# Causal pooling of three groups by transposes and doubled sums on VectorE instead of banded products

## The chip, the cores and the metric

The kernel runs on one core of one Trainium2 chip. The metric is the time of one execution on the device, in microseconds (us), as the median of several runs; lower is better. Each run is one layer of a decoder on 256 tokens of 2048 channels, in fp32.

A core has a matrix engine (TensorE, PE in the profile), a vector engine (VectorE, DVE), a scalar engine (ScalarE, ACT), a general engine (GpSimd, POOL) and a queue engine that issues most transfers (SyncE, SP). Each engine takes its own list of instructions in order, and semaphores tie the lists together. Products are summed in PSUM, a memory of eight banks.

## The reference

One input product gives, for each token, q, k, v, z (2048 columns each), two small sets for the heads, the pooling input p, and two gates g_a and g_b. q, k and v go through a causal convolution and then the gated delta rule (`gated_delta_rule`), whose output is normalized per head and gated by z. Beside it runs the pooling, in four groups of 512 channels with windows 2, 4, 8 and 16:

```
def causal_multiscale_pool(u):        # u: (B, S, G, Cg)
    cs = jnp.pad(jnp.cumsum(uf, axis=1), ((0, 0), (1, 0), (0, 0), (0, 0)))
    t = jnp.arange(seq)
    for gi, win in enumerate(POOL_WINDOWS):
        hi = cs[:, 1:, gi]
        lo = cs[:, jnp.maximum(t + 1 - win, 0), gi]
        cnt = jnp.minimum(t + 1, win).astype(jnp.float32)
        outs.append((hi - lo) / cnt[None, :, None])
    ...
    return (pooled - uf)
...
y_b = jnp.einsum('bsgc,gcd->bsgd', pooled, pool_w[l]).reshape(bsz, seq, D_POOL) * pool_scale[l]
mixed = jax.nn.sigmoid(g_a) * y_a + jax.nn.sigmoid(g_b) * y_b
```

So each token gets the mean over its last `win` tokens less itself, times a 512x512 matrix per group (`pool_w`). The rest of the layer is the output product and a gated MLP with 5632 hidden channels.

## The kernel before, in words

**Weights.** All matrices are fp32 and are used as two parts, a high part `whi` and a low part `wlo`. A weight tile is 256 rows by 512 columns. `srcs` lists all tiles in the order of use; SP issues their loads into four buffers `raw`; ScalarE casts `raw` to `whi` (L143) and VectorE subtracts it from `raw` to give `wlo` (L151), here called the split. `whi` and `wlo` have three buffers each. The activations are held in two parts too (`xhl`). `gemm_a` (L170 to L185) multiplies one tile into a pair of PSUM banks (`psm`) by 12 products of 128x512: high by high (L181), low by high (L182), high by low (L183), for two halves of the rows and two halves of the tokens. A product of 2048 rows takes eight tiles, one of `pool_w` two. There are two pairs of `psm` and four single banks `psg`.

**Order.** Work on the side is put between the weight products in two ways. Functions put into `later` run when the second tile of the next `gemm_a` begins. And after every six products `side()` takes one step of a generator, `gdn` (from L634), which holds the gated delta rule of the group: decays, gram products of q and k, the inverses of 32x32 blocks by many small VectorE steps (L744, L746), their doubling by small products, and the output. Each `yield` ends a step, and `LATE` and `WAIT` are counts of empty steps. The order in which each engine takes its instructions is then set by the build's planner, which goes by its own estimates of time and is not bound to the order of the text; only the start and, on PE, group 3's end are ordered by hand.

**Groups.** The loop at L864 runs over four groups of 512 channels. Each one multiplies k, q, v, p and the gate g_b, then `pool_w`, then z and g_a. Every result is scaled and evicted from PSUM to the tile `ev` by ScalarE (`evict`). k and q are turned (channels to partitions) by eight transposes on PE (`turned`, L226) and convolved there. v stays with tokens in the partitions; its convolution adds three copies moved by one to three tokens, which go through a DRAM tile (`vrow` stored at L883, `mv` loaded at L594, multiplied by the taps at L601, added at L602).

**Pooling.** `pooled` (L894 to L905) multiplies the evicted p by a band matrix (`bands`, one per group) that holds the mean's weights, 1/win or one over the count at the start, less the identity. It takes eight fp32 products (L899, L901), which the profile lists as two records each; the result is turned as it comes. ScalarE casts it to `phi` (L904) and VectorE takes `plo` from PSUM (L905), two halves each. The bands are made once by GpSimd and VectorE in `fixed_parts` (L534 to L548). The product with `pool_w` follows g_b's; its result is scaled by `pool_scale` (L918), then by one plus the tanh of g_b (L919). z's gate goes to `sz` (L923).

**The 0/1 product.** The normalization of q within the rule needs sums of q's squares per head and token. They are summed over 32 columns (`qp`, L725), then a product with a 0/1 matrix `sel` (L729) brings the parts together into `psg`, and four VectorE instructions (L733) scale them into `ro`, which the rule's end reads (L857). This stands ahead of the inverses' steps.

Of the kernel before, what the change touches and what calls it, by code (L numbers as in the profile page):

```python
# [7 lines left out]
F32 = mybir.dt.float32  # L8
# [5 lines left out]
P = 128  # L14
S = 256
# [19 lines left out]
def kernel(  # L35
# [492 lines left out]

    bands = mp.tile([P, 4, NB], F32, name="bands")

# [3 lines left out]
    def fixed_parts():  # L534
        for g, win in enumerate(WINDOWS):
            bd = bands[:, g, :]
            nc.gpsimd.memset(bd, 0.5 / win)
            nc.vector.tensor_copy(bd[:, 0:PAD], icnt[:, g, :])
            for cs in (slice(0, P + PAD), slice(P + PAD, NB)):
                b = bd[:, cs]  # L540
                n = cs.stop - cs.start
                nc.gpsimd.affine_select(b, b, pattern=[[1, n]], compare_op=ALU.is_ge, fill=0.0, base=0,
                                        channel_multiplier=-1)
                nc.gpsimd.affine_select(b, b, pattern=[[-1, n]], compare_op=ALU.is_ge, fill=0.0, base=win - 1,
                                        channel_multiplier=1)
                nc.vector.tensor_tensor(b[:, 0:P], b[:, 0:P], idh, op=ALU.subtract)
        nc.gpsimd.memset(Ta, 0.0)
        nc.gpsimd.memset(TTa, 0.0)  # L548
# [85 lines left out]
    def gdn(g, kq, vt, conv, res):  # L634
# [92 lines left out]
        yield  # L727
        pn = pg([P, 4, 2, 4])
        mm(pn.rearrange("p h t c -> p (h t c)"), sel.rearrange("p b i -> p (b i)"), qp, start=True, stop=True)  # L729
        ro = mp.tile([P, 2, 4], F32, tag="ro", name=nm("ro"))  # L730
        for c in range(4):
            pr = slice(32 * c, 32 * c + 32)
            nc.vector.tensor_scalar(ro[pr], pn[pr, :, :, c].rearrange("p h t -> p t h"), EPS * P, EPS * EPS * P,  # L733
                                    op0=ALU.mult, op1=ALU.add)
        for _ in range(WAIT - 3 + LATE[g]):
# [128 lines left out]
    for g in range(4):  # L864
# [24 lines left out]
        ps = gemm_a(xh, xl, KD)  # L889
        e = evict(ps)  # L890
        phi = mtile(g, [P, 4, S], F32R, nm("phi"))
        plo = mtile(4 + g, [P, 4, S], F32R, nm("plo"))

        def pooled(e=e, g=g, phi=phi, plo=plo):  # L894
            for f2 in range(2):
                pt = pg([P, 2, S])
                for ff in range(2):
                    fs = slice((2 * f2 + ff) * P, (2 * f2 + ff + 1) * P)
                    mm(pt[:, ff, P:S], e[:, 1, fs], bands[:, g, P + PAD : NB], start=True, stop=False,  # L899
                       skip_group_check=True)  # L900
                    mm(pt[:, ff, 0 : P + PAD], e[:, 0, fs], bands[:, g, 0 : P + PAD], start=False, stop=True,  # L901
                       skip_group_check=True)
                fs = slice(2 * f2, 2 * f2 + 2)
                nc.scalar.copy(phi[:, fs, :], pt)  # L904
                nc.vector.tensor_tensor(plo[:, fs, :], pt, phi[:, fs, :].bitcast(F32), op=ALU.subtract)  # L905

        later.append(pooled)

# [14 lines left out]
        nc.vector.scalar_tensor_tensor(sz, gate(ps, "th"), 1.0, ps, op0=ALU.add, op1=ALU.mult)  # L923
        if g == 3:
# [220 lines left out]
```

## Time and profile before

| | |
|---|---|
| median of 3 runs | 1565.36 us (1564.85 to 1565.47) |
| the profiled execution | 1565.06 us |
| its span in the profile | 1563.3 us |
| granted TensorE clock | 0.998 |
| PE busy | 1554.1 us, 99% |
| VectorE busy | 1085.6 us, 69% |
| ScalarE busy | 745.7 us, 48% |
| GpSimd busy | 41.3 us, 3% |
| read from HBM | 297.56 MB, 194 GB/s over the span |

The profile is one execution as the hardware profiler saw it. Its rows name a line of the kernel, an engine, an operation, and tiles in the form out<-in; a tile's name without its number stands for all of that name. In the views by time, a row has the start and the duration in us; x2 or x8 means that so many alike follow one another. Matmuls overlap: the time from one start to the next is shorter than the duration of one. The share of a DMA or engine is an average over the stretch named. "Idle before" is the time in which an engine had nothing to do just before an instruction, with what ended it.

### The profile page before, as it was taken

Reading aid. Unit: us, or ns where it says so; the run is one execution under the profiler, and the core shown is the slowest. Engines: PE = TensorE matmul, PEld = TensorE weight load, DVE = VectorE, ACT = ScalarE, POOL = GpSimd, SP = SyncE. Lnnn points to the kernel's source line nnn. Section 1 sums busy time; section 2 is a strip of 40 time slices with the busy share of each in tenths; the row PEclk is TensorE's granted clock in tenths of the full one; section 3 lists DMA queues with packets and bytes.
Section 4 is the critical chain, followed back from the end, with each engine's and each line's share of the span. In section 5 each row is a group of like instructions: output and inputs, shape, how many; then the busy total and the mean of one; then the engine's idle time right before and its main releaser. Section 6 shows DMA issues by size and latency. Waiting matters only on the chain.

```text
span 1563.3 us, 21270 instructions
## 1 busy us (share of the span) xinstructions
PE 1554.1 (99%) x8008; PEld 1306.1 (84%) x8008; DVE 1085.6 (69%) x1702; ACT 745.7 (48%) x958; POOL 41.3 (3%) x69
## 2 busy tenths in 40 slices
PE   9999999999999999999999999999999999999997
PEld 8878888888888888888888888888888888888886
DVE  6898758896698848886656666776666667444444
ACT  6545445454554445354544544444444444333443
POOL 2110000000000001000000000000000000000000
PEclk9999999999999999999999999999999999999999
DMA  8676657676676656676656666666666666666662
GB/s 273 200 222 207 194 162 212 201 208 178 182 221 198 194 152 201 210 209 184 212 180 177 196 187 188 188 190 188 187 184 195 188 188 214 197 191 210 200 223 91
DMA packets 168229, 304.23 MB, mean 195 GB/s; under 512 B 19234, under 2 KB 22834, under 8 KB 167998
## 3 DMA queue, kind: packets, MB, share of 16 engines
q1 hardware_dynamic: 165104, 297.84, 64.0%
q10 hardware_dynamic: 3022, 5.03, 0.9%
q8 instruction: 63, 1.03, 0.3%
q14 instruction: 40, 0.33, 0.1%
HBM read 297.56 MB, written 5.27 MB: 194 GB/s over the span
## 4 chain that ended last, share of the span: by engine, by line
PE 99%; issue 1%; ACT 0%; DVE 0%; POOL 0%; POOLq 0%
PE psm L183 15%; PE psm L181 15%; PE psm L182 15%; PE psm L205 10%; PE psg L205 10%; PE psg L206 5%; PE psm L206 5%; PE psg L1058 3%; PE psg L1060 2%; PE psg L1059 2%; PE psm L1059 2%; PE psm L1060 2%; PE psm L1058 2%; PE psm L312 1%; PE psg L673 1%; PE psg L226 1%
## 5 line engine op out<-in xcount | busy, mean ns | idle before, releaser
L151 DVE TENSOR_TENSOR wlo<-raw,whi 128x1024 fp32r<-128x1024 f32 x522 | 636.7, 1223 | 374.1 <-ACT whi L143 371.2
L143 ACT CAST whi<-raw 128x1024 fp32r<-128x1024 f32 x524 | 551.1, 1053 | 715.7 <-PE psm L182 314.9
L183 PE MATMUL psm<-wlo,xhl 128*128 128x512 f32 x864 | 339.8, 393 | 0.0
L182 PE MATMUL psm<-whi,xhl 128*128 128x512 f32 x864 | 338.9, 392 | 0.0
L181 PE MATMUL psm<-whi,xhl 128*128 128x512 f32 x864 | 338.0, 391 | 0.0
L205 PE MATMUL psm<-fhl,whi 128*128 128x512 f32 x704 | 246.2, 396 | 0.0
L205 PE MATMUL psg<-fhl,whi 128*128 128x512 f32 x704 | 238.0, 394 | 0.0
L206 PE MATMUL psm<-fhl,wlo 128*128 128x256 f32 x704 | 194.4, 279 | 0.0
L183 PEld LDWEIGHTS psm<-wlo,xhl 128*128 128x128 f32 x864 | 162.3, 188 | 33.1
L182 PEld LDWEIGHTS psm<-whi,xhl 128*128 128x128 f32 x864 | 162.2, 188 | 33.1
L181 PEld LDWEIGHTS psm<-whi,xhl 128*128 128x128 f32 x864 | 162.2, 188 | 32.7
L206 PE MATMUL psg<-fhl,wlo 128*128 128x256 f32 x704 | 178.7, 279 | 0.0
L205 PEld LDWEIGHTS psm<-fhl,whi 128*128 128x128 f32 x704 | 131.4, 188 | 30.5
L205 PEld LDWEIGHTS psg<-fhl,whi 128*128 128x128 f32 x704 | 129.2, 188 | 24.2
L206 PEld LDWEIGHTS psg<-fhl,wlo 128*128 128x128 f32 x704 | 132.5, 188 | 6.9
L206 PEld LDWEIGHTS psm<-fhl,wlo 128*128 128x128 f32 x704 | 132.5, 188 | 1.1
L1058 PE MATMUL psg<-whi,hhi 128*128 128x512 f32 x168 | 65.5, 390 | 0.0
L1059 PE MATMUL psg<-whi,hlo 128*128 128x512 f32 x168 | 65.4, 389 | 0.0
L1058 PE MATMUL psm<-whi,hhi 128*128 128x512 f32 x168 | 65.4, 389 | 0.0
L1059 PE MATMUL psm<-whi,hlo 128*128 128x512 f32 x168 | 65.4, 389 | 0.0
L1060 PE MATMUL psm<-wlo,hhi 128*128 128x512 f32 x168 | 65.4, 389 | 0.0
L1060 PE MATMUL psg<-wlo,hhi 128*128 128x512 f32 x168 | 59.0, 389 | 0.0
(267 smaller groups left out, 1519.0 us busy)
## 6 DMA issues: line engine op xcount, KB each, us to landing
raw<-in_w_in_dram SPq DMA_DIRECT2D x224, 512.0 KB, 4.3
raw<-in_w_up_dram SPq DMA_DIRECT2D x176, 512.0 KB, 4.5
raw<-in_w_down_dram SPq DMA_DIRECT2D x88, 512.0 KB, 4.4
raw<-in_w_out_dram SPq DMA_DIRECT2D x32, 512.0 KB, 4.7
mv<-vrow SPq DMA_DIRECT2D x12, 512.0 KB, 5.6
taps<-in_conv_qkv_w_dram SPq DMA_DIRECT2D x16, 256.0 KB, 5.1
raw<-in_pool_w_dram SPq DMA_DIRECT2D x8, 512.0 KB, 4.5
vrow<-ev SPq DMA_DIRECT2D x4, 512.0 KB, 3.0
```

Source lines behind the costliest of these rows:

```text
L143: nc.scalar.copy(hi, raw)
L151: last_split[0] = nc.vector.tensor_tensor(lo, raw, hi.bitcast(F32), op=ALU.subtract).ins
L181: mm(ps[:, t, :], lh(k, t), hi[:, kk, :], start=(k == 0), stop=False)
L182: mm(ps[:, t, :], ll(k, t), hi[:, kk, :], start=False, stop=False)
L183: mm(ps[:, t, :], lh(k, t), lo[:, kk, :], start=False, stop=(k == nk - 1))
L205: mm(ps[f], hi[:, kk, fs], rhl(k), start=(k == 0), stop=False, skip_group_check=True)
L206: mm(ps[f][:, 1, :], lo[:, kk, fs], rhl(k)[:, 0, :], start=False, stop=(k == nk - 1), skip_group_check=True)
L226: nc.tensor.transpose(pt[:, ff, t * P : (t + 1) * P], src[:, t, f * P : (f + 1) * P], ident)
L312: mm(ps_k0[:, t, :], part(k, t), w[:, kk, :], start=(k == 0 and w is hi and part is xh), stop=(k == KD - 1 and w is lo))
L1058: mm(acc[c][t], lh(k, t), hi[:, kk, :], start=(k == 0), stop=False)
L1059: mm(acc[c][t], ll(k, t), hi[:, kk, :], start=False, stop=False)
L1060: mm(acc[c][t], lh(k, t), lo[:, kk, :], start=False, stop=(k == KF - 1))
```

## The change

In groups 0, 1 and 2 the pooling is no longer a product with a band. The evicted p (now scaled by half the norm, `rsh`) is turned by eight transposes, ScalarE copies it out of PSUM, and VectorE forms the sum over the window by doubling: a tile plus itself moved by one column, then by two, then by four, so one addition for window 2, two for 4, three for 8. ScalarE copies the first columns that have no partner. The sum times 1/win, less the tile, is the pooled tile, with the first `win` columns done apart by the counts; ScalarE casts it to `phi`, and VectorE takes `plo` from it, both in one piece of 1024 a partition. Group 3, with window 16, keeps its band, and only that band is made.

In groups 0 to 2 the product with `pool_w` comes behind z's product, and the order of loads in `srcs` follows. `yb` is now formed first from the gate and `pool_scale`, then multiplied by the product. In all four groups the 0/1 product and its four scalings stand behind the inverses' last transfers, with one more `yield`. The tile `bat` of the start takes another buffer's name.

```diff
-        srcs += cols(pool_w[0, g], 0, 4)
-        for base in (C_Z, C_GA):
-            srcs += cols(w_in[0], base + 512 * g, KD)
+        parts = [cols(pool_w[0, g], 0, 4), cols(w_in[0], C_Z + 512 * g, KD)]
+        for part in parts if g == 3 else parts[::-1]:
+            srcs += part
+        srcs += cols(w_in[0], C_GA + 512 * g, KD)
...
-    nc.vector.tensor_scalar(icnt, icnt, 0.5, None, op0=ALU.mult)
...
-    bat = mp.tile([64, 2, S], F32, tag="u", name="bat")
+    bat = mp.tile([64, 2, S], F32, tag="w2", name="bat")
...
-    bands = mp.tile([P, 4, NB], F32, name="bands")
+    bands = mp.tile([P, NB], F32, name="bands")
...
     def fixed_parts():
-        for g, win in enumerate(WINDOWS):
-            bd = bands[:, g, :]
-            nc.gpsimd.memset(bd, 0.5 / win)
-            nc.vector.tensor_copy(bd[:, 0:PAD], icnt[:, g, :])
...
+        win = WINDOWS[3]
+        nc.gpsimd.memset(bands, 0.5 / win)
+        nc.vector.tensor_scalar(bands[:, 0:PAD], icnt[:, 3, :], 0.5, None, op0=ALU.mult)
...
-        pn = pg([P, 4, 2, 4])
-        mm(pn.rearrange("p h t c -> p (h t c)"), sel.rearrange("p b i -> p (b i)"), qp, start=True, stop=True)
-        ro = mp.tile([P, 2, 4], F32, tag="ro", name=nm("ro"))
-        for c in range(4):
-            pr = slice(32 * c, 32 * c + 32)
-            nc.vector.tensor_scalar(ro[pr], pn[pr, :, :, c].rearrange("p h t -> p t h"), EPS * P, EPS * EPS * P,
-                                    op0=ALU.mult, op1=ALU.add)
         for _ in range(WAIT - 3 + LATE[g]):
             yield
...
             nc.sync.dma_start(TTa[rs, :, rs], tbd.rearrange("(q r) a (c i) -> r (a c) q i", q=8, i=B0)[r])
+        pn = pg([P, 4, 2, 4])
+        mm(pn.rearrange("p h t c -> p (h t c)"), sel.rearrange("p b i -> p (b i)"), qp, start=True, stop=True)
+        ro = mp.tile([P, 2, 4], F32, tag="ro", name=nm("ro"))
+        for c in range(4):
+            pr = slice(32 * c, 32 * c + 32)
+            nc.vector.tensor_scalar(ro[pr], pn[pr, :, :, c].rearrange("p h t -> p t h"), EPS * P, EPS * EPS * P,
+                                    op0=ALU.mult, op1=ALU.add)
+        yield
...
-        e = evict(ps)
+        e = evict(ps) if g == 3 else evict(ps, rsh)
         phi = mtile(g, [P, 4, S], F32R, nm("phi"))
-        plo = mtile(4 + g, [P, 4, S], F32R, nm("plo"))
-
-        def pooled(e=e, g=g, phi=phi, plo=plo):
+        plo = []
+
+        def banded(e=e, g=g, phi=phi, plo=plo):
+            plo.append(mtile(4 + g, [P, 4, S], F32R, nm("plo")))
...
+        def pooled(e=e, g=g, win=win, phi=phi, plo=plo):
+
+
+            u = mp.tile([P, 4, S], F32, tag="pu", name=nm("pu"))
+            for f2, pt in enumerate(turned(e)):
+                nc.scalar.copy(u[:, 2 * f2 : 2 * f2 + 2, :], pt)
+            src, n = u, 1
+            while n < win:
+                if n * 4 == win:
+                    dst = mp.tile([P, 4, S], F32, tag="pa", name=nm("pa"))
+                else:
+                    dst = mtile(4 + g, [P, 4, S], F32, nm("pb"))
+                nc.scalar.copy(dst[:, :, 0:n], src[:, :, 0:n])
+                nc.vector.tensor_tensor(dst[:, :, n:], src[:, :, n:], src[:, :, : S - n], op=ALU.add)
+                src, n = dst, 2 * n
+            pool = mp.tile([P, 4, S], F32, tag="pa", name=nm("pool"))
+            nc.vector.tensor_tensor(pool[:, :, 0:win], src[:, :, 0:win],
+                                    icnt[:, g, 0:win].unsqueeze(1).to_broadcast([P, 4, win]), op=ALU.mult)
+            nc.vector.tensor_tensor(pool[:, :, 0:win], pool[:, :, 0:win], u[:, :, 0:win], op=ALU.subtract)
+            nc.vector.scalar_tensor_tensor(pool[:, :, win:], src[:, :, win:], 1.0 / win, u[:, :, win:],
+                                           op0=ALU.mult, op1=ALU.subtract)
+            nc.scalar.copy(phi, pool)
+            plo.append(mtile(4 + g, [P, 4, S], F32R, nm("plo")))
+            nc.vector.tensor_tensor(plo[0], pool, phi.bitcast(F32), op=ALU.subtract)
+
+        later.append(banded if g == 3 else pooled)
...
-        ps = gemm_a(lambda k, t: phi[:, k, t * P : (t + 1) * P], lambda k, t: plo[:, k, t * P : (t + 1) * P], 4)
         yb = mp.tile([P, 2, 512], F32, tag="yb", name=nm("yb"))
-        nc.vector.tensor_tensor(yb, ps, psb.unsqueeze(1).to_broadcast([P, 2, 512]), op=ALU.mult)
-        nc.vector.scalar_tensor_tensor(yb, tb, 1.0, yb, op0=ALU.add, op1=ALU.mult)
-
-        ps = gemm_a(xh, xl, KD)
-        sz = mp.tile([P, 2, 512], F32, tag="sz", name=nm("sz"))
-        nc.vector.scalar_tensor_tensor(sz, gate(ps, "th"), 1.0, ps, op0=ALU.add, op1=ALU.mult)
+        nc.vector.scalar_tensor_tensor(yb, tb, 1.0, psb.unsqueeze(1).to_broadcast([P, 2, 512]),
+                                       op0=ALU.add, op1=ALU.mult)
+        sz = None
+
+        for part in ("pool", "z") if g == 3 else ("z", "pool"):
+            if part == "pool":
+                ps = gemm_a(lambda k, t: phi[:, k, t * P : (t + 1) * P],
+                            lambda k, t: plo[0][:, k, t * P : (t + 1) * P], 4)
+                nc.vector.tensor_tensor(yb, yb, ps, op=ALU.mult)
+            else:
+                ps = gemm_a(xh, xl, KD)
+                sz = mp.tile([P, 2, 512], F32, tag="sz", name=nm("sz"))
+                nc.vector.scalar_tensor_tensor(sz, gate(ps, "th"), 1.0, ps, op0=ALU.add, op1=ALU.mult)
```

More of the change, by code (lines that the diff above doesn't have):

```diff
@@ L534, in fixed_parts @@
     def fixed_parts():
-        for g, win in enumerate(WINDOWS):
-            bd = bands[:, g, :]
-            nc.gpsimd.memset(bd, 0.5 / win)
-            nc.vector.tensor_copy(bd[:, 0:PAD], icnt[:, g, :])
[L539 to L546, printed above, removed]
+        win = WINDOWS[3]
+        nc.gpsimd.memset(bands, 0.5 / win)
+        nc.vector.tensor_scalar(bands[:, 0:PAD], icnt[:, 3, :], 0.5, None, op0=ALU.mult)
+        for cs in (slice(0, P + PAD), slice(P + PAD, NB)):
+            b = bands[:, cs]
+            n = cs.stop - cs.start
+            nc.gpsimd.affine_select(b, b, pattern=[[1, n]], compare_op=ALU.is_ge, fill=0.0, base=0,
+                                    channel_multiplier=-1)
+            nc.gpsimd.affine_select(b, b, pattern=[[-1, n]], compare_op=ALU.is_ge, fill=0.0, base=win - 1,
+                                    channel_multiplier=1)
+            nc.vector.tensor_tensor(b[:, 0:P], b[:, 0:P], idh, op=ALU.subtract)
         nc.gpsimd.memset(Ta, 0.0)
@@ L904, in pooled @@
                 nc.scalar.copy(phi[:, fs, :], pt)
-                nc.vector.tensor_tensor(plo[:, fs, :], pt, phi[:, fs, :].bitcast(F32), op=ALU.subtract)
-        later.append(pooled)
+                nc.vector.tensor_tensor(plo[0][:, fs, :], pt, phi[:, fs, :].bitcast(F32), op=ALU.subtract)
+        def pooled(e=e, g=g, win=win, phi=phi, plo=plo):
[21 more added lines that the diff above has]
+        later.append(banded if g == 3 else pooled)
         def gate(ps, tag):
```

4 lines of the change are left out of this document (2 added, 2 removed).

## The prediction

> **What bounds the kernel now.** I read the page's first rows, then the chain that ended last, then the waits of PE, then PE's timeline around the pooling, and only then VectorE's.
>
> ```profile
> span 1563.3 us, 21270 instructions
> PE 1554.1 (99%) x8008; PEld 1306.1 (84%) x8008; DVE 1085.6 (69%) x1702; ACT 745.7 (48%) x958; POOL 41.3 (3%) x69
> ...
> PE 99%; issue 1%; ACT 0%; DVE 0%; POOL 0%; POOLq 0%
> ```
>
> PE is busy for 99% of the span and makes 99% of the chain. The waits of PE hold one row:
>
> ```profile
> PE psm L242 <- POOL ones L232: 1.1, 1, 1.1
> ```
>
> That is the very first product. From there PE streams products with nothing between them that the profile calls a wait. So the time is the sum of what PE issues, and an edit counts in two ways only: it takes products out of that stream or puts some in, or it makes PE wait for a weight part. Each weight tile needs a cast on ScalarE (L143) and a subtraction on VectorE (L151, "the split"), and PE cannot take the tile's low part before its split has ended.
>
> **The sum is made against the profiled execution.** It took 1565.06 us, of which 1563.3 is its span; the median of the runs is 1565.36, 0.30 higher. 0.2% of it is 3.13 us, about what a measurement of this kernel can tell from no change.
>
> **PE's part.** Group 0's pooling, as PE issued it (start, duration):
>
> ```profile
> 125.37 0.39 PE L182 MATMUL psm<-whi,xhl 128*128 128x512 f32 x1
> 125.60 0.30 PE L729 MATMUL psg<-qp,sel 128*128 128x32 f32 x2
> 125.74 0.47 PE L899 MATMUL psg<-bands,ev 128*128 128x128 f32 x2
> ...
> 127.60 0.49 PE L183 MATMUL psm<-wlo,xhl 128*128 128x512 f32 x1
> 127.92 0.40 PE L181 MATMUL psm<-whi,xhl 128*128 128x512 f32 x1
> ```
>
> Weight products start 0.23 us apart (125.37 to 125.60). From the 0/1 product's start at 125.60 to 127.92 are 2.32 us, which hold one weight product: the inserted block costs 2.32 − 0.23 = 2.09 us, 0.14 of it for the 0/1 product (125.60 to 125.74), 1.95 for the eight banded products. What the change puts there stands in the trace already, as the turning of another evicted tile by eight transposes:
>
> ```profile
> 250.53 0.39 PE L183 MATMUL psm<-wlo,xhl 128*128 128x512 f32 x1
> 250.76 1.03 PE L226 MATMUL psg<-ident,ev 128*128 128x128 f32 x8
> 251.55 0.48 PE L181 MATMUL psm<-whi,xhl 128*128 128x512 f32 x1
> 251.86 0.40 PE L182 MATMUL psm<-whi,xhl 128*128 128x512 f32 x1
> L226 PE MATMUL psg<-ident,ev 128*128 128x128 f32 x64 | 9.1, 273 | 0.0
> ```
>
> 250.76 to 251.86, less one weight product, is 0.87 us. So each of groups 0, 1 and 2 saves 1.95 − 0.87 = 1.08 us of PE: 3.24 in all. Group 3 keeps its bands. One transpose is recorded with 273 ns, but eight of them start within 0.79 us, so they overlap; it is the spacing that the stream pays, and I take that. The clock in such stretches was full (1.00 in the window below). The Trainium skill, "TensorE: Matmul & The Clock Gate", section "Part 4: PE-mode transpose", gives about 275 ns for a 128x128 transpose in one kernel's context, mostly access latency, and says that transposes do not count as PE-busy in the same way for the gate. This trace agrees on the duration (273) and shows no loss of clock.
>
> The **0/1 product** now comes by itself, behind the inverses, in all four groups, in a place of its own between weight products. The nearest row for a small block by itself:
>
> ```profile
> 74.85 0.40 PE L659 MATMUL psg<-r,lowr 128*128 128x256 f32 x2
> 75.09 0.40 PE L182 MATMUL psm<-whi,xhl 128*128 128x512 f32 x1
> ```
>
> Two larger products took 0.24 us together, so a change of operands costs little. By itself the 0/1 product costs between 0.14, as in its block, and its recorded 0.30: 0 to 0.16 more, four times 0 to 0.64. I take 0.06 each, nearer the small block, 0.25 in all. PE's part: −3.24 + 0.25 = −3.0 (−2.6 to −3.25). The four scalings of its result (L733) and its wait move with it; what reads them, the norm of the output, comes long after.
>
> **VectorE's and ScalarE's part.** Rows by line:
>
> ```profile
> L151 DVE TENSOR_TENSOR wlo<-raw,whi 128x1024 fp32r<-128x1024 f32 x522 | 636.7, 1223 | 374.1 <-ACT whi L143 371.2
> L143 ACT CAST whi<-raw 128x1024 fp32r<-128x1024 f32 x524 | 551.1, 1053 | 715.7 <-PE psm L182 314.9
> L905 DVE TENSOR_TENSOR plo<-psg,phi 128x512 fp32r<-128x512 f32 x8 | 5.2, 686 | 0.1
> L904 ACT CAST phi<-psg 128x512 fp32r<-128x512 f32 x8 | 4.7, 586 | 4.6 <-PE psg L901 4.6
> L923 DVE SCALAR_TENSOR_TENSOR sz<-gate,psm 128x1024 f32<-128x1024 f32 x4 | 4.9, 1214 | 0.0
> L602 DVE TENSOR_TENSOR vt<-vt,mv 128x1024 f32<-128x1024 f32 x12 | 14.6, 1215 | 0.0
> L733 DVE TENSOR_SCALAR ro<-psg 32x8 f32<-32x8 f32 x16 | 2.6, 162 | 0.5
> L791 ACT COPY U<-psg 32x128 f32<-32x128 f32 x16 | 4.1, 258 | 0.8 <-PE psg L788 0.4
> L546 DVE TENSOR_TENSOR bands<-bands,idh 128x128 f32<-128x128 f32 x8 | 2.4, 305 | 0.0
> ```
>
> Added on VectorE: 1 + 2 + 3 doubling adds of up to 1024 a partition, as L602, 6 × 1.22 = 7.3; per group one subtraction with scale as L923, one split of the pooled tile as L151, and two corrections of the first columns as L733: 3 × (1.21 + 1.22 + 0.32) = 8.3. Removed: six splits as L905, 4.1. Net +11.5 us. ScalarE: six copies of the evicted turned tile take the place of six casts of the same shape (0.59 each); added are three casts of 1024 (1.05) and six small copies of first columns (at most 0.26): +4.7. The fixed part shrinks to a quarter: six subtractions of L546 and three small copies leave VectorE, about 2 us, before group 0's pooling, and GpSimd (3% busy) loses the like. The doubled rows are one long chain that alternates between the two engines, and on each it queues among casts and splits.
>
> All of that lies beside PE's products, as long as the splits stay ahead. How full VectorE is (columns: length; PE, weight load, VectorE, ScalarE, GpSimd busy; clock; DMA share; GB/s), and how far ahead a split is:
>
> ```profile
> 475.00:505.00 30.00, 30.00 (x142) 25.16 (x142) 26.06 (x46) 14.43 (x16) 0.00 (x0) 1.00 0.65 188
> 516.32 1.23 DVE L151 TENSOR_TENSOR wlo<-raw,whi 128x1024 fp32r<-128x1024 f32 x1
> 519.05 1.23 DVE L151 TENSOR_TENSOR wlo<-raw,whi 128x1024 fp32r<-128x1024 f32 x1 [0.40 <-ACT whi L143]
> 521.16 0.39 PE L183 MATMUL psm<-wlo,xhl 128*128 128x512 f32 x1
> ```
>
> In the steady stretch splits are 2.73 us apart, PE's pace for a tile. The split that ends at 517.55 is used at 521.16: a lead of 3.61, which three buffers don't let grow. Group 2, around 475 to 505, is the tightest place: VectorE is busy for 26.06 of 30 us, and that is where three doublings go, among the inverses' small steps (L744, L746). In the changed kernel's queue, by the durations above, the work from split to split there is 4.1, 2.95, 2.93, 2.94, 2.93, 2.91, then 2.05 us. Out of a lead of 3.61 the first costs 1.38, the next five about 1.05 together; five hand-overs at an estimated 0.1 leave a lead of about 0.7. Group 1 has 4.1, 2.61, 2.97, 2.14, 2.93, 2.91, from an estimated start near 2.8: about 0.9 at the least. Group 0, with one doubling, keeps over 2. No stall there, by this sum. The pooled tile itself is not late: its product now comes behind z's eight tiles (8 × 2.73 = 21.8 us) and part of the gate's, some 31 us after the transposes, while the longest chain has about 12 us of work. In return z's sum must leave its bank before the g_a product starts, two pool_w tiles (5.5 us) after z's end: two tanh (taken at L904's 0.59) and one L923 (1.21) are 2.4 us, and behind a cast and a split at worst (2.3) they still fit, with 0.8 to spare. SP's loads of pool_w and z change places with it; they are alike.
>
> **Group 0's convolution of v** is the place where the moved instructions bite. It stands ahead of the pooling, but the planner orders it anew, since VectorE's time before it has changed. In the changed queue the first tap product (L601), which waits for a DMA, comes ahead of the split for the product's sixth tile, with the gram reductions and further tap products behind it. Group 0, then the same wait in group 2:
>
> ```profile
> 86.95 0.37 SPq L883 DMA_DIRECT2D vrow<-ev  x1
> 97.69 2.56 DVE L601 TENSOR_TENSOR mv<-mv,taps 128x1024 f32<-128x1024 f32 x2 [2.42 <-DMA mv<-vrow]
> 103.94 0.39 PE L183 MATMUL psm<-wlo,xhl 128*128 128x512 f32 x1
> 444.32 0.37 SPq L883 DMA_DIRECT2D vrow<-ev  x1
> 452.77 1.23 DVE L601 TENSOR_TENSOR mv<-mv,taps 128x1024 f32<-128x1024 f32 x1 [2.38 <-DMA mv<-vrow]
> ```
>
> If the rows land as before, at 97.69, the queue behind (loads of 5.7 and about 1.9 us) brings the split's end to 105.24 where PE wants it at 103.94: a stall of 1.3 us. If they land as in group 2, 8.45 us after the store's issue, that is at 95.40, nothing is lost. The third of these copies is issued ahead of two weight loads in the changed queue, and VectorE is freer before it, so I lean to the second: 0.3 (0 to 1.5).
>
> **The sum**: −3.0 + 0.3 = −2.7. The profiled run 1562.36, the median 1562.7 us.
>
> **Rivals.**
>
> *The whole gain and nothing lost.* The 0/1 product is free as in its block, group 0 loses nothing, and perhaps freer VectorE time before group 0 gives back a little: −3.24, 1562.1. For it: the overlap of small products above. Against it: the new order in group 0.
>
> *Slower: PE waits for splits behind the doubling chain.* Each hand-over of the chain to ScalarE can queue behind a cast of 1.05 and take a copy of up to 0.26, and VectorE, which takes its queue in order, holds the splits behind its waiting add. Nine hand-overs (2, 3 and 4 in groups 0 to 2) at 1.31, less the leads of 2.3, 0.9 and 0.7: 0.3 + 3.0 + 4.5 = 7.8. With −3.0 that is +4.8, 1570.2. It decides once hand-overs use up more than the leads; more than 3.0 us of stalls makes the kernel slower. For it: leads under 1 us and an engine at 26.06 of 30. Against it: ScalarE's 48%, and casts that mostly wait for PE ("PE psm L182 314.9"), so that they are not themselves late.
>
> *Group 0 stalls in full*: −3.0 + 1.5, 1563.9. For it: a landing at 97.69; against it the earlier issue.
>
> *Transposes cost what is recorded*: 8 × 0.273 = 2.18 against 1.95, +0.23 per group, +0.7, and 0.25 for the 0/1 product: 1566.3. The rows' spacing (0.79 us for eight) speaks against it. The section of the Trainium skill named above prices a transpose at this duration.
>
> **How the numbers follow.** The forecast has 0.45, of which 0.11 lies beyond −3.13 (below 1562.23); the whole gain 0.26; slower by hand-overs 0.19, of which 0.13 lies past +3.13 (1568.49), since its hand-overs are alike and come together; group 0 in full 0.06; costly transposes 0.04. Faster: 0.26 + 0.11 = 0.37. Slower: 0.13. The same: 0.34 + 0.06 + 0.06 + 0.04 = 0.50. The predicted time is the forecast's, 1562.7, whose own range is 1562.1 to 1564.2. The range of 8 in 10 runs from 1561.6, under the whole gain by the scatter of the runs, up to 1567.0, which takes in the small stalls and the costly transposes and leaves the larger stalls out.
>
> **What the profile of the changed kernel would show.** The banded group (L899, L901) with 8 products each in place of 32, 24 more transposes, PE's busy time about 3 us less, and no gap in PE's spacing of 0.23. Right at each pooling block: about 1.1 us between the neighbouring weight products where 2.3 were. Wrong on the 0/1 product if its block costs over 0.2. A gap of PE near 104 us would be the v convolution's stall; gaps near 310 to 320 and 495 to 504 the doubling chain's, with split rows whose idle time is put down to ScalarE. A wait at the g_a product's start would be z's bank. The prediction fails if such gaps sum to over 3 us, or if the planner's new order moves a stall to a place that I haven't read.

## The result and the profile after

The changed kernel takes 1562.95 us (median of 22 runs) where the kernel before, run beside it, takes 1565.47: a ratio of 0.9983, 95% interval 0.9977 to 0.9989. That is 2.5 us less, not more than 0.2%. The forecast was 1562.7 in a range of 1561.6 to 1567.0, and "the same" had the largest chance. The time is right. The sum behind it is not: one term was about right, one of the small ones did not come, and a wait of 1.1 us that was not in it came instead.

The first row and the busy times on the changed kernel's page (engine, busy us, share of the span, instructions):

```profile
span 1561.0 us, 21220 instructions
PE 1550.9 (99%) x7984; PEld 1303.1 (83%) x7984; DVE 1091.5 (70%) x1704; ACT 748.8 (48%) x967; POOL 53.4 (3%) x54
```

PE's busy time fell by 3.2 us, VectorE's rose by 5.9, and the span fell by 2.3 only. Where the difference went is in the waits of PE (engine, tile, line, what it waited for: us in total, times, the longest), which had one row before:

```profile
PE psm L243 <- POOL ones L233: 1.1, 1, 1.1
PE psg L788 <- DVE T L765: 0.7, 1, 0.7
```

The second row is new: the first doubling of the inverses (L788) waits for the transposed blocks `T` (L765). It happens in group 3 alone. The timeline there, PE's rows and VectorE's, before:

```profile
718.91 0.39 PE L183 MATMUL psm<-wlo,xhl 128*128 128x512 f32 x1
719.23 0.69 PE L788 MATMUL psg<-T,ga 32*32 32x32 f32 x32
719.85 0.50 PE L181 MATMUL psm<-whi,xhl 128*128 128x512 f32 x1
...
716.40 1.84 DVE L765 STREAM_TRANSPOSE T<-TT 32x256 f32<-32x256 f32 x4 [3.14 <-DMA TT<-tbd]
```

and after:

```profile
715.32 0.39 PE L184 MATMUL psm<-wlo,xhl 128*128 128x512 f32 x1
715.83 0.24 PE L788 MATMUL psg<-T,ga 32*32 32x32 f32 x2
716.77 0.69 PE L788 MATMUL psg<-T,ga 32*32 32x32 f32 x30 [0.69 <-DVE T L765]
717.38 0.50 PE L182 MATMUL psm<-whi,xhl 128*128 128x512 f32 x1
...
715.35 1.84 DVE L765 STREAM_TRANSPOSE T<-TT 32x256 f32<-32x256 f32 x4 [2.96 <-DMA TT<-tbd]
```

Before, the last transpose ended at 718.24 and PE came at 719.23: 1 us to spare. After, PE comes at 715.83, 3.4 us sooner, and the transposes only 1.05 sooner. From the last weight product to the next one the block takes 717.38 − 715.32 = 2.06 us where it took 719.85 − 718.91 = 0.94: 1.1 us lost.

The other end of the inverses' chain on VectorE, its first step in group 3, before and after:

```profile
667.32 0.42 DVE L744 TENSOR_TENSOR tmp<-lb,tb 128x248 f32<-128x248 f32 x1 [3.03 <-DMA lb<-cdd]
...
665.16 0.42 DVE L736 TENSOR_TENSOR tmp<-lb,tb 128x248 f32<-128x248 f32 x1 [1.99 <-DMA lb<-cdd]
```

The chain begins 2.16 us sooner. From there to the end of the last transpose it takes 52.0 us where it took 50.9, with the four scalings of the 0/1 product (L752, 0.68 us at 668.71) now inside it. So the chain follows PE by 1.05 us out of 3.4, the 1 us to spare is used up, and the rest is the wait.

The pooling blocks themselves are nearly as the prediction had them. Group 1 after:

```profile
300.01 1.03 PE L227 MATMUL psg<-ident,ev 128*128 128x128 f32 x8
...
301.12 0.39 PE L182 MATMUL psm<-whi,xhl 128*128 128x512 f32 x1
...
301.58 0.30 PE L748 MATMUL psg<-qp,sel 128*128 128x32 f32 x2
...
302.03 0.39 PE L182 MATMUL psm<-whi,xhl 128*128 128x512 f32 x1
```

The transposes: 300.01 to 301.12, less a product of 0.23, 0.88 us. The 0/1 product: 301.58 to 302.03, less 0.23, 0.22. Taken from the spacing of the neighbouring products over the whole of PE's stream, the blocks cost 0.89 and 0.24 against 2.11 before, so each of groups 0 to 2 saves 0.98; in group 3 the band's block is 1.89 and the 0/1 product 0.24, 0.02 more than before. Together −2.92. With the new wait, +1.14, that is −1.78; PE's start is 0.22 sooner, and the second doubling's products of group 2 (L808) stand in one block of 16 where they stood in two of 8, which costs 0.34 less (the change aims at neither). That makes −2.34, and the span fell by 2.3.

Beside the tight stretch of group 2, VectorE and ScalarE after (columns as in the prediction):

```profile
475.00:505.00 30.00, 30.00 (x139) 24.96 (x138) 27.71 (x41) 18.25 (x28) 0.00 (x0) 1.00 0.69 196
499.22 1.21 DVE L152 TENSOR_TENSOR wlo<-raw,whi 128x1024 fp32r<-128x1024 f32 x1
501.63 0.39 PE L184 MATMUL psm<-wlo,xhl 128*128 128x512 f32 x1
```

VectorE is busy for 27.71 of 30 us, and the smallest lead behind the pooling is 501.63 − 500.43 = 1.2 us. No weight product waits for a split.

### The profile page after: what moved, and what is told of

Its sections match the earlier page's. It is cut to its first block, busy times and chain, and to the rows that moved or that the text cites. A ratio compares the mean times of both kernels' runs of the same rounds, so it can differ in the third digit from the quotient of the medians.

```text
span 1561.0 us, 21220 instructions
## 1 busy us (share of the span) xinstructions
PE 1550.9 (99%) x7984; PEld 1303.1 (83%) x7984; DVE 1091.5 (70%) x1704; ACT 748.8 (48%) x967; POOL 53.4 (3%) x54
## 3 DMA queue, kind: packets, MB, share of 16 engines
q8 instruction: 62, 1.02, 0.3%
## 4 chain that ended last, share of the span: by engine, by line
PE 98%; issue 1%; DMA 0%; DVE 0%; ACT 0%; SPq 0%; POOL 0%; POOLq 0%
PE psm L182 15%; PE psm L184 15%; PE psm L183 15%; PE psm L206 11%; PE psg L206 10%; PE psg L207 5%; PE psm L207 5%; PE psg L1090 3%; PE psg L1092 3%; PE psg L1091 2%; PE psm L1092 2%; PE psm L1091 2%; PE psm L1090 2%; PE psm L313 1%; PE psg L672 1%; PE psg L227 1%
```

## The experiments

Times are medians; each stands beside runs of the kernel before on the same chip, whose median is given. Positions in PE's stream are counted in tiles: the weight products ahead of a row, as the trace lists them, divided by 12.

### The 0/1 product put back, and a later step in group 3

First: is the new wait due to the four scalings (L752) that now stand in the inverses' chain, or to the transfers of the blocks? And does a later step on PE take it away?

```diff
 # e1, and e3 with the second edit too
+        pn = pg([P, 4, 2, 4])
+        mm(pn..., sel..., qp, start=True, stop=True)      # and the four scalings, ahead of the empty steps
         for _ in range(WAIT - 3 + LATE[g]):
             yield
...
-        pn = pg([P, 4, 2, 4])
-        ...
-        yield
 # e2 and e3
         if g == 3:
             yield
+            yield
```

> The changed kernel with the 0/1 product and its four scalings put back ahead of the inverses in all four groups. Theory A (the 1.14 us that PE loses at group 3's first doubling comes from the four scalings of 0.17 us that now stand inside the inverses' chain on VectorE, beside what else was moved there): the gap shrinks by about 0.7 us, to 0.3 to 0.6, and the product costs about 0.14 with its neighbours in place of 0.24 by itself, 0.1 in each group; about 1.0 us less than the changed kernel, 1561.9 us. Theory B (the gap comes from the small transfers of the 32x32 blocks, which land late behind weight loads): the gap stays at about 1.1, and the time falls by 0.4 at most, 1562.5.

Measured: 1567.11 us beside 1565.62; ratio 1.0005 (0.9996 to 1.0014). The whole gain is gone. The profiled execution's waits of PE:

```profile
PE psg L787 <- DVE T L764: 2.8, 2, 2.1
```

The block at the first doubling costs 3.92 us in place of 0.84 (measured like the blocks above, less the products' own spacing). The profiled execution took 1564.83 us with a mean granted clock of 0.998, the slowest of the eleven 1567.63 with 0.996; what the median has beyond the wait is not in this trace. Both theories fall: the wait did not shrink by 0.7 nor stay, it grew threefold. VectorE's rows in group 3 suggest why:

```profile
650.83 1.22 DVE L724 TENSOR_REDUCE qp<-kq 128x32 f32<-128x1024 f32 x1
...
655.52 0.47 DVE L696 SCALAR_TENSOR_TENSOR ga<-psg,sj,dec 128x256 f32<-128x256 f32 x1
...
668.61 0.42 DVE L743 TENSOR_TENSOR tmp<-lb,tb 128x248 f32<-128x248 f32 x1 [2.35 <-DMA lb<-cdd]
```

With the 0/1 product ahead of the inverses, the planner also places the reduction of q's squares (L724) ahead of the last gram scalings (L696). These end at 655.99, their transfer (`cdd`, `lb`) follows, and the inverses' chain begins at 668.61. In the changed kernel L696 stands ahead of L724, and the chain begins at 665.16. Of these 3.45 us, 2.1 are the scalings' later end (653.85 in the changed kernel) and 1.3 the longer way through the transfer. So the move of the 0/1 product, which the prediction priced at a loss of 0.25 us, is what holds the wait at 1.1 us here. By itself beside the transposes the product costs 1.07 − 0.89 = 0.17 us, so moving it costs 0.06, the figure predicted.

> The changed kernel with one more empty step in group 3 ahead of the first doubling, so that PE reaches it six products (1.36 us) later. Theory A and B alike: the gap of 1.14 us at the first doubling goes, since the transposed blocks came 0.69 us late after the first two products and PE lost 1.14 in all; 1561.8 us. Rival: the steps behind it are as tight as the first one, and the wait turns up at the end of the rule, ahead of the output product; 1562.9 or more.

Measured: 1562.11 us beside 1565.62; ratio 0.9978 (0.9969 to 0.9986); span 1560.0, the lowest here.

```profile
716.88 0.39 PE L184 MATMUL psm<-wlo,xhl 128*128 128x512 f32 x1
717.19 0.69 PE L789 MATMUL psg<-T,ga 32*32 32x32 f32 x32
717.82 0.50 PE L182 MATMUL psm<-whi,xhl 128*128 128x512 f32 x1
...
715.08 1.84 DVE L765 STREAM_TRANSPOSE T<-TT 32x256 f32<-32x256 f32 x4 [2.49 <-DMA TT<-tbd]
```

The transposes end at 716.92 and PE comes at 717.19: no wait, and the block is back to 0.94. The span is 1.0 us under the changed kernel's, which is the wait. As times the two kernels' intervals overlap, so the gain over the changed kernel is shown by the trace, not by the timing.

> Both edits together: the 0/1 product back ahead of the inverses and one more step in group 3. Theory A: no gap left at the first doubling and 0.1 us less in each group for the product, 1561.4 us, about 4.0 below the kernel before. Theory B: the same time, since the later step hides the transfers too. Rival (the steps behind are as tight): 1562.5.

Measured: 1564.08 us beside 1565.62; ratio 0.9991 (0.9982 to 1.0). The block at the first doubling still costs 2.90, a wait of 2.1. One step moved the wait by 1.0, as in e2, and the 2.1 left are the chain's late begin. Theory B's "the later step hides the transfers too" and theory A's "no gap left" are both wrong.

### The two other parts of the change

```diff
 # e4: the changed kernel
-        for part in parts if g == 3 else parts[::-1]:
+        for part in parts:
...
-        for part in ("pool", "z") if g == 3 else ("z", "pool"):
+        for part in ("pool", "z"):
 # e5: the kernel before, its 0/1 product moved as in the change
 # e6: the kernel before, z and pool_w exchanged as in the change
```

> The changed kernel with the pool_w product ahead of z's again in groups 0 to 2, loads too. In the changed kernel's trace group 2's pooled parts end at 491.71 (high) and 493.21 (low), and its pool_w product could start 21.8 us earlier than it does, at 490.3. Theory: PE waits there for about 2.5 to 3 us in group 2, in group 1 (parts at 310.67, product at 312.2) and group 0 hardly at all: 1565.5 us, the whole gain gone. Rival: the planner places the chain earlier, or leads absorb it: 1562.9, as the changed kernel.

Measured: 1575.79 us beside 1565.62; ratio 1.0065 (1.0054 to 1.0077).

```profile
PE psg L788 <- DVE T L765: 3.3, 2, 2.6
PE psm L183 <- DVE plo L931: 2.0, 2, 1.0
PE psm L182 <- ACT phi L929: 1.6, 2, 1.1
```

The theory is right in kind and short in size. In the profiled execution (1573.36 us) PE waits for the pooled parts in group 1 (2.6 us more between its products there) and in group 2 (1.9), then 3.6 more than its due at the first doubling in group 3; and after the first and last of these the products run slowly for some 3 us, about 1.5 us each time (last section). The exchange is what makes the longer chain of the pooling free.

> The kernel before with only the 0/1 product and its scalings moved behind the inverses, bands kept in all groups. Theory C (formed after the product was put back: with the 0/1 product ahead, the squares of q stand ahead of the last gram scalings on VectorE, and the inverses' chain in group 3 begins 3.4 us later; the move buys that time): group 3's chain begins 2 to 3 us earlier than before, against the first doubling's place on PE, which had about 1 us to spare; no wait either way; PE pays 0.06 to 0.1 us in each group for the product by itself; 0.2 to 0.4 above the kernel before, 1565.9. Rival (the move itself makes group 3 late): a wait of about 1 us at the first doubling, 1566.9.

Measured: 1565.61 us beside 1565.52; ratio 1.0002 (0.9993 to 1.0011). No wait, and no time that could be told. The banded block without the 0/1 product costs 1.89 and the product by itself 0.24, 2.13 against 2.11: the move costs 0.02 in each group. But theory C falls as a general statement: the chain in group 3 begins at 667.74, where it began at 667.32 before. The move by itself does not start the chain earlier; it does so only in the order that the planner finds with the new pooling. The rival is half right, though. The chain ends later:

```profile
719.66 0.44 DVE L766 STREAM_TRANSPOSE T<-TT 32x256 f32<-32x256 f32 x1
...
719.96 0.69 PE L789 MATMUL psg<-T,ga 32*32 32x32 f32 x32
```

The last transpose ends at 720.10, when PE has begun at 719.96; before, it ended 1 us ahead of PE. So the move alone uses up what group 3 had to spare. The same move costs time to spare in the kernel before and gains it in the changed one.

> The kernel before with only z's product ahead of pool_w's in groups 0 to 2 (loads and yb with it), bands and 0/1 product as before. Theory: the pooled parts of the band are ready within a few us, so nothing waits and nothing is saved: the same as the kernel before within 0.5 us, 1565.6. Rival: the g_a product waits for z's bank, 1 us or more in each group: 1568 or above.

Measured: 1565.02 us beside 1565.52; ratio 0.9995 (0.9986 to 1.0003): the same. PE has one more wait, 0.2 us for a split in group 0 (at 109 us). No wait for z's bank, and at group 3's first doubling the time to spare is kept (transposes end at 717.98, PE comes at 719.20).

### What makes group 3 late

In the changed kernel group 2's first doubling comes at tile 175.9 of PE's stream (before: 173.9), and group 3's first gram products at 202.2 (before: 199.9), while group 3's first doubling is held by the order written by hand at tile 231.0 in both. So from its first gram products to its first doubling group 3 has 2.3 tiles, 6 us, less. The chain of its inverses does not begin later for that: it begins 2.16 us sooner, since the last gram scalings end at 653.85 where they ended at 655.68.

```diff
 # e7: e2, and
-                nc.vector.tensor_tensor(dst[:, :, n:], src[:, :, n:], src[:, :, : S - n], op=ALU.add)
+                for _ in range(2):
+                    nc.vector.tensor_tensor(dst[:, :, n:], src[:, :, n:], src[:, :, : S - n], op=ALU.add)
 # e8: e2, and group 3 like the others
-                if n * 4 == win:
+                if n * 4 == win or n * 16 == win:
...
-        later.append(banded if g == 3 else pooled)
+        later.append(pooled)
 # e9 (g in (2, 3)) and e10 (g in (1, 3)): the changed kernel, two bands, and
-        later.append(banded if g == 3 else pooled)
+        later.append(banded if g in (2, 3) else pooled)
 # likewise for the order of pool_w and z
```

> The changed kernel with the later step, and each doubling addition issued twice, 1.22 us more VectorE work in group 0, 2.44 in group 1, 3.66 in group 2. Theory (leads are what pays): with the later step group 2's smallest leads in its pooling are 0.6 to 0.9 us, so PE waits there for about 3 us; group 1, with more lead, for 0 to 0.6, group 0 not at all: 1562.1 + 3 to 3.6 = 1565.4. Rival (VectorE has 4 us in 30 to spare, so the work fits): 1562.1. Rival (hand-overs between the engines price each addition at more than its own work): 1567 or above.

Measured: 1572.74 us beside 1565.52; ratio 1.0046 (1.0032 to 1.006). The added work costs 10.6 us over e2, and most of it not where it was added:

```profile
PE psg L789 <- DVE T L765: 6.7, 2, 6.1
...
PE psm L184 <- DVE wlo L152: 0.4, 1, 0.4
```

Waits for splits come to 0.4 us in the whole run. Group 2's first doubling moved on to tile 181.7 and group 3's first gram product to 207.2, and group 3, which has no addition, waits at its fixed place: from the last weight product to the next the block takes 8.36 us in place of 0.94, 7.4 lost. Then PE runs at a granted clock of 0.50 until 730.9, which costs about 2 us more. The theory that leads are what pays is wrong: the planner puts the rule's steps on PE later when VectorE has more to do, and few splits are late. In group 3 the chain begins at 676.71, 11 us later than in e2, so here the delay does reach the one place that cannot move.

> The changed kernel with the later step, and group 3 too by transposes and four doublings, its pool_w product behind z's. PE saves another 1.0 us. Theory (what counts in group 3 is the inverses' chain ahead of the first doubling): VectorE gets about 6 us more in that stretch, the chain ends some 5 us later, and PE waits at the first doubling for 4 to 6 us: 1566. Rival (the chain is put ahead of the pooling and the work beside it is hidden): 1561.1.

Measured: 1570.36 us beside 1565.52; ratio 1.0031 (1.0019 to 1.0043).

```profile
PE psg L789 <- DVE T L765: 6.9, 2, 6.3
```

As the theory says, only more: the chain ended at 715.3 in place of 707.9 in e2, and the block at the first doubling takes 8.58 us in place of 0.94, 7.6 lost, with a granted clock of 0.50 from 718.7 to 728.9, about 2 us more. In group 3, in this order, there is no room for the doubling.

> The changed kernel with group 2 kept on its band, pool_w ahead of z there as before (groups 0 and 1 by transposes). Theory D (formed from the positions in PE's stream: in the changed kernel group 2's first doubling comes at tile 175.9 in place of 173.9 and group 3's first gram product at 202.2 in place of 199.9, while group 3's first doubling is held at tile 231.0; the three additions of group 2 delay its inverses, and the delay is collected in group 3): the positions go back to about 174 and 200, the wait at group 3's first doubling goes, PE saves 2 x 0.98: 1563.6, about 0.6 above the changed kernel though a third of the saving is given up. Rival (the wait comes from the sum saved on PE, whichever group saves it): a wait of about 0.2 to 1 stays, 1564.5.

Measured: 1566.26 us beside 1565.49; ratio 1.0001 (0.9992 to 1.001). The first half of theory D holds: the positions went back to 173.9 and 199.9. No wait is left at the first doubling either, but the time did not follow:

```profile
PE psm L184 <- DVE wlo L152: 1.5, 3, 0.6
...
685.68 0.50 PE L184 MATMUL psm<-wlo,xhl 128*128 128x512 f32 x1 [0.61 <-DVE wlo L152]
...
720.82 0.69 PE L788 MATMUL psg<-T,ga 32*32 32x32 f32 x32
...
680.36 1.22 DVE L152 TENSOR_TENSOR wlo<-raw,whi 128x1024 fp32r<-128x1024 f32 x1
...
681.76 1.22 DVE L606 SCALAR_TENSOR_TENSOR vt<-th,vt 128x1024 f32<-128x1024 f32 x1
683.01 1.22 DVE L951 TENSOR_TENSOR yb<-yb,psm 128x1024 f32<-128x1024 f32 x1
...
684.41 1.22 DVE L152 TENSOR_TENSOR wlo<-raw,whi 128x1024 fp32r<-128x1024 f32 x1
...
720.08 0.44 DVE L765 STREAM_TRANSPOSE T<-TT 32x256 f32<-32x256 f32 x1
```

Now it is the splits in group 3 that are late: 4.05 us from one to the next at 680.36, with the end of v's convolution and `yb`'s product between. PE loses 0.8 + 1.9 us to splits between 638 and 690, where the kernel before loses next to none. Late splits are what the slower rival feared, though not from its hand-overs and in a group that it did not name. And they are why nothing waits at the first doubling: PE comes there at 720.82, 1.6 us later than in the kernel before. The last transpose ends at 720.52, and the chain begins at 668.34, over 3 us later than in the changed kernel (717.19 and 665.16; PE's later start is 0.65 of it). So with the positions back where they were the chain is no sooner, and the second half of theory D is not shown.

> The changed kernel with group 1 kept on its band, pool_w ahead of z there as before (groups 0 and 2 by transposes). Theory D: group 2's delay stays, its first doubling at about tile 176 and group 3's first gram product at 202; a wait of about 1.1 us at group 3's first doubling, PE saves 2 x 0.98: 1564.7. Rival (the additions of groups 1 and 2 share the delay): half the wait, 1564.1.

Measured: 1565.52 us beside 1565.49; ratio 1.0004 (0.9995 to 1.0013). The positions are those of the changed kernel (175.9 and 202.2), and the wait is there, 1.6 us in the block; 0.4 us went to a split as well. With e9 it ties the positions to group 2's pooling, not to the sum saved. It does not tie group 3's wait to them: the chain begins at 667.25 here, 2.1 us later than in the changed kernel (PE's later start is 0.2 of it), at the same positions.

What in group 2's pooling moves group 2's first doubling? The additions have an alibi in the changed kernel's own rows:

```profile
481.27 1.22 DVE L921 TENSOR_TENSOR pb<-pu 128x1020 f32<-128x1020 f32 x1
482.60 1.22 DVE L921 TENSOR_TENSOR pa<-pb 128x1016 f32<-128x1016 f32 x1
...
485.07 1.20 DVE L921 TENSOR_TENSOR pb<-pa 128x1008 f32<-128x1008 f32 x1
487.44 0.42 DVE L736 TENSOR_TENSOR tmp<-lb,tb 128x248 f32<-128x248 f32 x1 [1.17 <-DMA lb<-cdd]
...
489.01 1.18 DVE L927 SCALAR_TENSOR_TENSOR pool<-pb,pu 128x992 f32<-128x992 f32 x1
...
492.00 1.22 DVE L931 TENSOR_TENSOR plo<-pool,phi 128x1024 fp32r<-128x1024 f32 x1
```

They fill the time in which VectorE waits for `lb` anyway. The subtraction (L927) and the split of the pooled tile (L931) stand inside the inverses' chain, which takes from 487.44 to 534.55 (47.1 us, 18 splits among it) where it took 489.31 to 532.3 (43.0 us, 16 splits). The last run tests it:

```diff
 # e12: e2, and
-                nc.vector.tensor_tensor(dst[:, :, n:], src[:, :, n:], src[:, :, : S - n], op=ALU.add)
+                (nc.gpsimd if g == 2 else nc.vector).tensor_tensor(dst[:, :, n:], src[:, :, n:], src[:, :, : S - n], op=ALU.add)
```

> The changed kernel with the later step, and group 2's three doubling additions on GpSimd in place of VectorE (3.66 us less on VectorE at its fullest stretch; GpSimd is 3% busy). The pooled tile may be later, since its product comes some 34 us after the transposes. Theory D: group 2's first doubling comes at tile 174 to 175 in place of 175.9 and group 3's rule one to two tiles earlier; either nothing waits then, 1562.1, or group 3's gram products fall among the splits as with the band in group 2, and PE loses 1 to 3 us there: 1563 to 1565. Rival (GpSimd's additions slow VectorE down, or take so long that the pooled tile is late): waits of the pool_w product on its parts in group 2, 1564 or more.

Measured: 1565.42 us beside 1565.97; ratio 0.9996 (0.9987 to 1.0005). Group 2's first doubling stays at tile 175.7: taking the additions off VectorE moves nothing there, so their time on VectorE is not the delay, and theory D as it was written here is wrong on that point. Group 3's chain begins 3 us later than in e2 (668.7 to 665.7), and the block at its first doubling takes 3.44 us in place of 0.94, part of it at a granted clock of 0.50 that holds from 720.2 to 723.6. That the subtraction and the split of the pooled tile are what delays group 2 is what remains; no run took them out of the chain alone, so it is argued from the rows and not shown.

What sets the begin of group 3's chain stays open. It is 665.2 in the changed kernel and 665.7 in e2, but 667.0 to 668.7 in the kernel before and in e1, e3, e5, e6 and e9 to e12, without following the positions; PE's own start differs by no more than 0.9 between these runs.

### How far the steps can be moved

```diff
 # e11: e1, and
         if g == 3:
             yield
+            yield
+            yield
+            yield
```

> The 0/1 product back ahead of the inverses, and three more empty steps in group 3 ahead of the first doubling (4.1 us of PE's stream; one step left a wait of 2.1 us). Theory: no wait at the first doubling, and the steps behind it still end in time; PE pays 0.17 us for the product beside the transposes in place of 0.24: 1561.9, as the changed kernel with one step more or 0.2 less. Rival (the end of the rule is the next thing to be late): the wait turns up between the rule's end and the output product, 1563 to 1565.

Measured: 1563.53 us beside 1565.49; ratio 0.9987 (0.9978 to 0.9996).

```profile
760.67 1.03 PE L227 MATMUL psg<-ident,sz 128*128 128x128 f32 x8
762.22 0.73 PE L182 MATMUL psm<-whi,mhi 128*128 128x512 f32 x2 [0.52 <-ACT mhi L992]
763.60 0.50 PE L183 MATMUL psm<-whi,mlo 128*128 128x512 f32 x1 [0.64 <-DVE mlo L993]
```

The rival is right. No wait is left at the first doubling; 1.5 us are lost at the rule's end, where the output product needs group 3's mixed tile (`mhi`, `mlo`) right behind its transposes. One step later is free, three are not.

## Why the prediction was right, and where it was not

**What bounds the kernel.** Right: the time is what PE issues and what PE waits for. Every difference between the traces above shows in the spacing of PE's products.

**PE's part.** Right. Predicted −3.0, measured −2.92. The transposes cost 0.89 (0.87 taken), by their spacing and not by their 273 ns, so the rival of costly transposes is out. Two terms were off and nearly cancelled. The three groups save 3 × (1.89 − 0.89) = 3.00 where 3.24 was taken, because the banded products by themselves cost 1.89 and not 1.95. The 0/1 product's move costs 0.08 in all where 0.25 was taken: by itself the product costs 0.24, but beside the bands it was 0.22 of the block's 2.11 and not 0.14 (e5). The prediction had named a block of over 0.2 as the sign of being wrong on this product, and that sign came, at 0.22 to 0.24.

**VectorE and ScalarE beside PE.** Right for groups 0 to 2: no split late, a smallest lead of 1.2 us in group 2's pooling where 0.7 was worked out. The slower rival's price for hand-overs did not come up. The pooling's work was put right: its rows on VectorE rise by 11.4 us (11.5 taken). The busy time rose by 5.9 only: the making of the bands and counts loses 3.0 (2 taken), and rows of the start that no edit touches (`rsh`, `rsq`, `r`) take 2.3 less. ScalarE's busy time rose by 3.1 (4.7 taken). GpSimd was to lose about 2 us and gained 12.1: the bands' rows fall by 7.5, but the 16 selections on `dec` (L663) take 1.53 us each in place of 0.61; no product waits for them. But the step "all of that lies beside PE's products, as long as the splits stay ahead" is the one that failed. It took the leads of the splits as the only way in which VectorE's work can reach PE. There is a second one: the inverses' chain runs on VectorE too, PE needs its end, and in group 3 PE's place for it is fixed by hand. The fixed order is told ahead of the prediction; that it had 1 us to spare (718.24 against 719.23) was not read. Taking 3 us out of PE's stream brings that place nearer by as much (3.4 us with the rest), while the chain's end comes only 1.05 sooner; the wait is 1.14 us in the changed kernel, and e2 shows what it is worth. Why the chain does not follow is shown in part: the move of the 0/1 product alone uses up the time to spare (e5), but with the new pooling undoing it makes the chain later still (e1).

**The pooled tile is not late.** Right, and needed: without z ahead of it PE waits for it in groups 1 and 2 (e4). The margin of z's bank held.

**Group 0's convolution of v.** 0.3 us were put in for a stall near 104 us; PE's products there are 0.23 apart. Nothing was lost; the lean to an earlier landing was right, and the term should have been 0.

**The 0/1 product.** The cost of its move was right to within 0.04 in each group (0.02 out of the bands' block, 0.06 from beside the transposes; 0.06 taken). Its worth was missed: put back, it costs 2 us of wait in group 3 (e1), by way of the planner's order. "The norm of the output comes long after" was true and not the point.

**The sum.** −2.92, +1.14 and −0.56 that the change did not aim at (the start's −0.22, the blocks of L808 −0.34) come near −2.7 by cancelling. A right total stands on a missing term of over a third its size, and that it came within 0.2 us is luck. The text did name "a stall to a place that I haven't read" as what would make it fail; that place exists, and it was small.

## What to carry to other kernels

When one engine's stream is shortened, look for every place where it meets another engine's chain at a fixed position, and read the spare time there from the trace first: that chain doesn't get shorter with it. Work added to an engine with spare time does not have to show where it is added; where a planner orders the queues, it moves other work later and the bill comes at the next thing that can't move. Parts of a change that look like costs alone may be what keeps the others' price down, and only undoing them one by one tells.

## What the runs showed of the hardware

Short waits of PE can be followed by a lower clock. In e4 PE stood still twice, 1.14 and 1.02 us, within 4 us, and then ran its products 0.43 us apart for 3 us (columns as in the prediction; the clock is the third number from the end):

```profile
311.00:315.00 4.00, 1.86 (x7) 0.97 (x6) 3.13 (x6) 2.60 (x4) 0.00 (x0) 0.96 0.79 244
315.00:318.40 3.40, 3.38 (x9) 2.70 (x10) 3.37 (x6) 0.56 (x1) 0.00 (x0) 0.55 0.65 177
```

The trace puts the clock at 0.50 from 314.66 to 318.07, 3.41 us; a mean of 0.55 over 3.4 us costs about 1.5 us more. In e12 waits of 1.12 and 0.69 us were followed by 0.50 from 720.21 to 723.63, 3.42 us. In e1's profiled execution PE waited longer, 2.05 and 0.72 us, and the clock stayed at 1.00:

```profile
715.00:718.50 3.50, 1.18 (x7) 0.57 (x5) 1.24 (x4) 1.04 (x1) 0.00 (x0) 1.00 0.71 180
718.50:722.00 3.50, 3.04 (x41) 2.58 (x42) 2.08 (x3) 1.03 (x4) 0.00 (x0) 1.00 0.55 142
```

The Trainium skill, "TensorE: Matmul & The Clock Gate", section "What's actually happening", describes a window of about 3.4 us that runs freely and lowers the clock after an idle one. The length of the slow spells (3.41 and 3.42 us) agrees, and that similar waits come out differently fits a window that does not start with the wait, though no run here shows where a window lies; but PE was not idle for the whole of any 3.4 us in e4, so the drop asks for less than the page says.

GpSimd's additions of the same tiles took 2.04, 1.88 and 2.74 us in e12, where VectorE's take 1.22. They end in time for the pooled tile, and still e12 is no faster. The length of one and the same GpSimd instruction varies more widely: in the changed kernel the 16 selections on `dec` (L663, 128x256) take from 0.40 to 4.99 us. What stretches them no run here shows.
